# Borders of the feed forward and the embedding gate: memory homes, first banks and queue order of the next stage's preparations

## The chip, the cores and the metric

The kernel runs on one core of a Trainium2 chip. The metric is the device time of one execution in microseconds (us). A core has five engines with a queue each: TensorE (PE), VectorE (DVE), ScalarE (ACT), GpSimd (POOL) and SyncE (SP), which here issues all transfers. Each works through its queue in order; instructions of different queues wait for one another by semaphores. Products land in PSUM, eight banks of 128 x 512 float32; all else is in SBUF, 224 KB per partition.

## The reference

A block of two layers on 1024 tokens of width 1024, in float32. Layer 0 mixes tokens with a gated convolution beside attention over the 256 best keys of each query, layer 1 with a gated delta rule. After its mixer each layer has a feed forward and an embedding gate:

```python
for i in range(DEPTH):
    hn = rmsnorm(h, norm_mix_g[i])
    h = h + mixer(hn, ...)                      # layer 0: convolution and attention; layer 1: delta rule
    h = h + swiglu(rmsnorm(h, norm_ffn_g[i]), ffn_w_gate[i], ffn_w_up[i], ffn_w_down[i])
    e = rmsnorm(p[i] @ ple_w_proj[i], ple_post_norm_g[i])
    h = h + e * jax.nn.sigmoid(rmsnorm(h, ple_norm_g[i]) @ ple_w_gate[i])
```

`swiglu(h, g, u, d)` is `(silu(h @ g) * (h @ u)) @ d`, with an inner width of 2816.

## The kernel before

**Precision.** Every large product is made of three products of halves: `split` (lines 107 to 109) has ACT round a tile to a high half and DVE subtract it from the source for the low half.

**Feed forward, gate and up (`ffn`, `ffn_gu`).** The products of 2 x 2 blocks are made with seven block products instead of eight. The normalized rows, transposed and split, give eight operands: B11, B21, B22 and the sums T1 to T4 (T1 = B12 - B11 and so on), each a pair of 8 KB tiles. `right` lays each pair out in a pool of its own. Weights come by `weights(n)` for the blocks n = 0 to 21: a load into one of two buffers `wr`, four POOL sums (`wino`, lines 779 to 781), then splits by ACT and DVE. `group(n, x)` runs the seven products on the bank tiles a, b and c and sums them on ACT and DVE; line 867 is the sum that must have read bank a before the product with T4 may add to it. `first_group` does the same for n = 0 while it still transposes the operands (line 882). For each pair of blocks j = 0 to 10, lines 931 to 933 multiply the gate by the up part; line 933 reads the last bank a. The result goes to DRAM (gfD) with four POOL sums Sg.

**Feed forward, down (`ffn_down`).** Four units of 2, 3, 3 and 3 inner pairs, each of seven steps. A step loads its slot from gfD (line 997, SP), splits it (lines 1002 and 1003), adds the split weights (line 109), runs 6 or 9 products into each of four banks of chain a or b (line 1013), and moves the banks into h: the first time by an ACT copy (line 1018), later by a DVE addition (line 1016). The chains of the seven steps are a, b, b, a, b, a, a. The weights' sums T_dn are made on POOL. The slots s0, s1, s2 and a fourth are used in turn. Beside it, from the second unit on, one row tile per step of the residual is loaded from hB (line 1023) and added to h by POOL (line 1024).

**Embedding gate (`ple`).** `weights(u)` loads two buffers, has ACT round them (line 1111) and POOL subtract (line 1112), into w0 for u = 0 and w1a, w1b for u = 1. `norm(t)` scales a row tile by DVE (line 203), PE transposes it, and ACT and DVE split it into hh and hl. `gate(u, t, w)` runs 24 products per bank (line 1131), a sigmoid, a product with the loaded e and an addition into h. The norms of the even row tiles get the priority of the last step of down.

**What sets the order.** The builder walks the traced program by priority, which is the order of the source unless `high_priority` says otherwise, and puts each instruction into its engine's queue when, by its own model of the time, it is ready. So an instruction whose inputs are ready may stand ahead of older ones. `self.after([ins])` queues what its block traces on the engine of `ins` behind `ins`; it adds an order and no wait.

**Memory homes.** Pools are laid out one behind another on the left side of SBUF, others on the right. A new tile waits for the last users of the tiles that lay at its address. In layer 0, from address 19.9 KB on, the feed forward has (in KB, worked out by adding up the tile sizes): B11 19.9, T1 35.9, the split weights 51.9, T2 83.9, B21 99.9, the weights' sums 116.9, B22 132.9, the gate and up tiles 148.9, the tags Tb 166.9 and Ta 174.9. Attention had its output weights at 19.9 to 51.9 and kT at 68.4 to 100.4. Down then has, in layer 0: s0 19.9 to 43.9, raw weights 51.9 to 75.9, s1 83.9 to 107.9, s2 107.9 to 131.9, T_dn sums 132.9 to 148.9, the fourth slot 148.9 to 172.9. The embedding gate has w0 at 99.9 to 131.9 in both layers, on s1 and s2. PSUM: gate and up use two banks for a, two for b, four for transposes; down uses four for a and four for b, and the tag that a pool uses first gets the lower four.

## Time and profile before

| | |
|---|---|
| three executions | 2999.12, 3006.69 and 3008.4 us, median 3006.69 |
| profiled execution | 2999.78 us; its span from first to last instruction 2998.0 us |
| busy, share of the span | PE 96%, DVE 62%, ACT 42%, POOL 36% |
| mean granted clock of PE | 0.984 |
| chain that ended last | PE 76%, DVE 10%, POOL 4%, issue 3%, ACT 3%, DMA 3% |
| transfers | 340.80 MB, mean 114 GB/s |

The span is what the views of the trace cover; 1.8 us of the execution lie around it. A stretch of the trace is given in us from the start of the span. The stages in it: layer 0's mixer to about 690, gate and up to 1131, down to 1357, embedding gate to 1459, layer 1's mixer to 2220, gate and up to 2662, down to 2891, embedding gate to the end.

### The profile page before, as it was taken

The numbers are of one execution on the slowest core, as the hardware profiler recorded it, in microseconds if no ns is written. First come the engines' busy times: TensorE is split into PE (matmuls) and PEld (weight loads), VectorE is DVE, ScalarE is ACT, GpSimd is POOL, SyncE is SP. The second block draws the span as 40 slices with busy tenths as digits, with TensorE's granted clock in tenths as the row PEclk, the third lists the DMA queues.
The fourth block names the chain that finished last, engine by engine and source line by source line (L and its number), as shares of the span: only waits on it lengthen the run. The fifth ranks groups of instructions, "written<-read, shape, count | busy, mean of one in ns | idle before, by whom it ended". The sixth has DMA issues, their size and how long they took to land.

```text
span 2998.0 us, 47759 instructions
## 1 busy us (share of the span) xinstructions
PE 2873.8 (96%) x19211; PEld 2391.8 (80%) x19211; DVE 1870.4 (62%) x3274; ACT 1255.2 (42%) x2225; POOL 1072.6 (36%) x931
## 2 busy tenths in 40 slices
PE   7999998999999998999999999999999999999999
PEld 6989876787888886787887777788678888877877
DVE  5799995565444448974466767664455444469861
ACT  4467725454333334333444455443233333344341
POOL 1341000123444437525212443342144444466342
PEclk9999999999999999999999999999999999999999
DMA  4122165201322236523332232223612322255422
GB/s 145 50 50 92 57 197 203 86 22 39 113 105 102 106 119 217 188 95 121 103 124 101 93 110 97 90 92 119 253 63 78 107 104 106 105 194 192 144 72 95
DMA packets 119822, 340.80 MB, mean 114 GB/s; under 512 B 11696, under 2 KB 34608, under 8 KB 101936
## 3 DMA queue, kind: packets, MB, share of 16 engines
q1 hardware_dynamic: 119600, 337.74, 32.8%
q8 instruction: 151, 2.47, 0.3%
q14 instruction: 71, 0.58, 0.1%
HBM read 240.64 MB, written 97.06 MB: 113 GB/s over the span
## 4 chain that ended last, share of the span: by engine, by line
PE 76%; DVE 10%; POOL 4%; issue 3%; ACT 3%; DMA 3%; SPq 0%; DVEq 0%; ACTq 0%; POOLq 0%
PE pga L850 16%; PE pgb L850 8%; PE pso L1362 7%; PE pda L1013 6%; PE pdb L1013 5%; PE psp L1131 5%; PE psz L216 4%; PE pgc L850 4%; PE psow L237 3%; PE psz L1622 2%; PE pskqv L227 2%; PE y L742 2%; PE pswob L237 2%; DVE sc L467 1%; PE pse L1043 1%
## 5 line engine op out<-in xcount | busy, mean ns | idle before, releaser
L1013 PE MATMUL pda<-sl 128*128 128x512 f32 x1008 | 237.9, 394 | 19.1 <-DVE g L933 7.4
L1013 PEld LDWEIGHTS pda<-sl 128*128 128x128 f32 x1008 | 190.3, 190 | 63.1 <-DVE g L933 8.3
L781 POOL TENSOR_TENSOR S<-wr_gu 128x512 f32<-128x512 f32 x44 | 68.4, 1555 | 398.1 <-DMA wr_gu<-in_w_gu_dram 380.5
L1013 PE MATMUL pdb<-sl 128*128 128x512 f32 x792 | 185.4, 392 | 1.3 <-DVE h L1016 1.3
L1013 PEld LDWEIGHTS pdb<-sl 128*128 128x128 f32 x792 | 149.8, 189 | 33.9 <-DVE h L1016 1.3
L109 DVE TENSOR_TENSOR w2l_gu<-S,w2h_gu 128x1024 fp32r<-128x1024 f32 x44 | 66.7, 1517 | 165.0 <-ACT w2h_gu L108 164.8
L1362 PE MATMUL pso<-hh,wl_od 128*128 128x512 f32 x384 | 157.6, 410 | 0.0
L1362 PE MATMUL pso<-hh,wh_od 128*128 128x512 f32 x384 | 156.8, 408 | 0.0
L1362 PE MATMUL pso<-hl,wh_od 128*128 128x512 f32 x384 | 156.6, 408 | 0.0
L1002 ACT CAST sl<-sl 128x1536 fp32r<-128x1536 f32 (+1 forms) x54 | 74.7, 1386 | 134.4 <-DMA sl<-gfD 134.3
L108 ACT CAST w2h_gu<-S 128x1024 fp32r<-128x1024 f32 x44 | 46.2, 1051 | 188.6 <-PE pga L850 94.0
L1003 DVE TENSOR_TENSOR sl<-sl 128x1536 fp32r<-128x1536 f32 (+1 forms) x54 | 107.7, 1999 | 27.9 <-ACT sl L1002 27.6
L1380 DVE SCALAR_TENSOR_TENSOR c<-pso,odcw,c 128x509 f32<-128x509 f32 (+1 forms) x144 | 107.0, 743 | 26.1 <-ACT c L1377 24.3
L779 POOL TENSOR_TENSOR T_dn<-wr_dn 128x512 f32<-128x512 f32 x44 | 78.7, 1817 | 97.5 <-PE pgb L850 52.3
L227 PE MATMUL pskqv<-wh_kqv,hh 128*128 128x256 f32 x384 | 109.5, 285 | 0.3 <-ACT wh_kqv L108 0.3
L227 PE MATMUL pskqv<-wh_kqv,hl 128*128 128x256 f32 x384 | 108.7, 283 | 0.0
L227 PE MATMUL pskqv<-wl_kqv,hh 128*128 128x256 f32 x384 | 108.3, 283 | 0.0
L603 DVE TENSOR_SCALAR_CACHE_REDUCE tk_junk<-sc,tk_f 128x1024 int8<-128x1024 f32 (+5 forms) x111 | 102.5, 924 | 1.8
L153 POOL TENSOR_SCALAR nss_f<-nss_f 128x1 f32<-128x1 f32 x16 | 3.1, 192 | 276.0 <-ACT junk_f L152 276.0
L1131 PE MATMUL psp<-wh_pg,hh_p 128*128 128x512 f32 x256 | 101.6, 397 | 0.0
L1131 PE MATMUL psp<-wl_pg,hh_p 128*128 128x512 f32 x256 | 100.5, 392 | 0.0
L1131 PE MATMUL psp<-wh_pg,hl_p 128*128 128x512 f32 x256 | 100.3, 392 | 0.0
(543 smaller groups left out, 9027.3 us busy)
## 6 DMA issues: line engine op xcount, KB each, us to landing
wr_gu<-in_w_gu_dram SPq DMA_DIRECT2D x44, 1024.0 KB
sl<-gfD SPq DMA_DIRECT2D x42, 768.0 KB
gfD<-Sg SPq DMA_DIRECT2D x22, 1024.0 KB
wr_dn<-in_w_dn_dram SPq DMA_DIRECT2D x22, 1024.0 KB
wr_od<-in_w_qkv_dram SPq DMA_DIRECT2D x12, 1024.0 KB
cD<-c SPq DMA_DIRECT2D x24, 512.0 KB
gfD<-g SPq DMA_DIRECT2D x22, 512.0 KB
wr_z<-in_w_z_dram SPq DMA_DIRECT2D x10, 1024.0 KB
```

What stands on the lines that cost most here:

```text
L216: nc.tensor.matmul(ps[:M, f * 512:(f + 1) * 512], a[:, kc, c], b[f][:, kc, :], start=(kc == 0 and i == 0), stop=(kc == KC - 1 and i == 2))
L227: nc.tensor.matmul(out, a[:, kc, c], b[:, kc, :], start=(kc == 0 and i == 0), stop=(kc == KC - 1 and i == 2))
L237: nc.tensor.matmul(ps[:, f * 512:(f + 1) * 512], a[:, kc, tsl], b[:, f * 512:(f + 1) * 512], start=(kc == 0 and i == 0), stop=(kc == nk - ...
L603: v.tensor_scalar(jk[:, :n], sc[b], fb, 0.0, op0=op, op1=ALU.add, accum_out=c)
L779: sub = lambda o, x, y: eng.tensor_tensor(o, x, y, op=ALU.subtract)
L850: nc.tensor.matmul(bank, a[:, kc, :], b[:, kc, :], start=first and kc == 0 and m == 0, stop=kc == 3 and m == 2, skip_group_check=True)
L1002: nc.scalar.copy(y, x.bitcast(F32))
L1003: v.tensor_tensor(x, x.bitcast(F32), y.bitcast(F32), op=ALU.subtract)
L1013: nc.tensor.matmul(ps, a[:, i, c], b[:, i, :], start=first and i == 0 and k == 0, stop=i == m - 1 and k == 2, skip_group_check=True)
L1131: nc.tensor.matmul(ps, a[:, kc, c], b, start=kc == 0 and i == 0, stop=kc == KC - 1 and i == 2)
L1362: nc.tensor.matmul(ps[:, f * 512:(f + 1) * 512], a[:, kc, :], b[f][:, kc, :], start=(kc == 0 and i == 0), stop=(kc == KC - 1 and i == 2))
L1380: nc.vector.scalar_tensor_tensor(c[:, e:(f + 1) * 512], ps[:, e - d:(f + 1) * 512 - d], cw[:, k:k + 1], c[:, e:(f + 1) * 512], op0=ALU.mul ...
```

## The change

1. Layer 0's attention remembers its last copy of transposed probabilities (`last_pT`, on DVE), and `first_group` of layer 0 traces `weights(0)` behind it.
2. In layer 0 the operand pairs change places: T1 and T2 at 19.9 to 51.9, B11 and B21 at 83.9 to 115.9. Layer 1 keeps its order.
3. The tags Ta and Tb of gate and up get a pool each, in the same order.
4. In the last pair of blocks, lines 931 and 932 are queued behind the last group's line 867 (`last_sum`).
5. In down, the four banks of chain b of the first unit are taken before those of chain a.
6. The residual rows are loaded and added at the overall steps 9, 11, ... 23 instead of 7 to 14.
7. The embedding gate lays its pools out in the order hh0, hl0, hh1, hl1, w1a, w1b, e, a pad, w0, in both layers. In layer 0 that puts w1a at 83.9, w1b at 99.9, e at 115.9 and w0 at 132.9 to 164.9 KB; layer 1 has the same addresses, since both start at 19.9.

```diff
-                        eng(pT[:, q4:q4 + m, :].rearrange("p a b -> p (a b)"), p[:, :m * P])
+                        mark = eng(pT[:, q4:q4 + m, :].rearrange("p a b -> p (a b)"), p[:, :m * P])
+                    self.last_pT = mark.ins
...
-            right(("B11", "T1"), "h1")
+            right(("B11", "T1") if l else ("T1", "T2"), "h1")
             if not l:
                 self.W2 = self.pool(es, f"ffn{l}w")
-            right(("T2", "B21"), "h2")
+            right(("T2", "B21") if l else ("B11", "B21"), "h2")
...
-            tp_ = self.pool(es, f"ffn{l}t")
-            self.ffn_gu(sp, fp, tp_, l, H, gD, right)
+            tb_ = self.pool(es, f"ffn{l}t")
+            ta_ = self.pool(es, f"ffn{l}u")
+            self.ffn_gu(sp, fp, {"Ta": ta_, "Tb": tb_}, l, H, gD, right)
...
-            w1, w2 = weights(0)
+            with self.after(None if l else [self.last_pT]):
+                w1, w2 = weights(0)
...
-            v.tensor_tensor(g[:, 0], u[:, 0], g[:, 0], op=ALU.mult)
-            v.tensor_tensor(g[:, 1, 1], u[:, 1, 1], g[:, 1, 1], op=ALU.mult)
+            with self.after([self.last_sum] if j == NFF // 2 - 1 else None):
+                v.tensor_tensor(g[:, 0], u[:, 0], g[:, 0], op=ALU.mult)
+                v.tensor_tensor(g[:, 1, 1], u[:, 1, 1], g[:, 1, 1], op=ALU.mult)
             v.tensor_tensor(g[:, 1, 0], last, g[:, 1, 0], op=ALU.mult)
...
             banks = {}
+            if not ui:
+                for tp in range(4):
+                    banks["b", tp] = self.tp(f"pdb{l}_0_1_{tp}", "b")
...
-                    if first:
+                    if first and (ui or chain == "a"):
                         banks[chain, tp] = self.tp(f"pd{chain}{nm}_{tp}", chain)
...
-                t = next(rest, None) if ui else None
+                t = next(rest, None) if 7 * ui + si in range(9, 25, 2) else None
...
-            hh = [x("hh0")]
-            fp = mk("e")
-            if l:
-                w1 = [mk("w1a")]
-                hl = [x("hl0")]
-                self.pad(es, 8, f"plp0{l}")
-            else:
-                self.pad(es, 8, f"plp0{l}")
-                hl = [x("hl0")]
-                w1 = [mk("w1a")]
+            hh, hl = [x("hh0")], [x("hl0")]
             hh.append(x("hh1"))
-            w0 = mk("w0")
-            self.pad(es, 1, f"plp1{l}")
             hl.append(x("hl1"))
             hT = [hh, hl]
-            w1.append(mk("w1b"))
+            w1 = [mk("w1a"), mk("w1b")]
+            fp = mk("e")
+            self.pad(es, 9, f"plp0{l}")
+            w0 = mk("w0")
```

## Rows read from the trace of the kernel before

**Rows 1.** Busy time of each engine over the span, from the page.

```profile
PE 2873.8 (96%) x19211; PEld 2391.8 (80%) x19211; DVE 1870.4 (62%) x3274; ACT 1255.2 (42%) x2225; POOL 1072.6 (36%) x931
```

**Rows 2.** Waits of PE over the span: engine line, waited for, us in total, times, longest us.

```profile
PE tp_p L193 <- DVE hn_p L203: 9.5, 6, 2.2
...
PE pda L1013 <- DVE g L933: 7.4, 2, 6.9
...
PE pda L1013 <- DVE h L1016: 7.4, 7, 2.7
...
PE tp_f_B L882 <- DVE HB11l L109: 5.4, 3, 2.0
...
PE pda L1013 <- ACT h L1018: 3.3, 1, 3.3
```

**Rows 3.** Stretches: us, length, busy by engine (rows 1's order), PEclk, DMA share, GB/s.

```profile
670.95:684.60 13.65, 11.22 (x41) 9.80 (x42) 4.33 (x7) 2.48 (x3) 5.13 (x4) 0.50 0.23 78
...
1138.58:1148.82 10.24, 6.20 (x15) 4.90 (x16) 5.35 (x7) 1.62 (x3) 9.62 (x8) 0.50 0.40 132
...
1363.86:1367.27 3.41, 2.89 (x11) 2.70 (x12) 3.41 (x7) 1.47 (x3) 3.41 (x2) 0.50 0.87 308
...
2691.64:2698.47 6.83, 5.06 (x12) 4.00 (x13) 5.62 (x6) 2.88 (x6) 5.99 (x4) 0.50 0.98 312
...
2896.44:2903.27 6.83, 4.94 (x16) 4.26 (x17) 6.62 (x9) 4.39 (x8) 6.67 (x5) 0.50 0.47 155
```

**Rows 4.** Timeline, attention to feed forward, layer 0: start, us, instruction, count, idle before.

```profile
667.37 2.23 DVE L109 TENSOR_TENSOR w1l_gu<-wr_gu,w1h_gu 128x1024 fp32r<-128x1024 f32 x1
...
671.92 1.12 PE L734 MATMUL tpp<-cf,L 128*128 128x128 f32 x4 [2.49 <-DVE pT L736]
...
672.83 5.22 PE L742 MATMUL y<-vv,pT 128*128 128x64 f32 x24
...
678.09 0.69 DVE L675 TENSOR_TENSOR yR<-y,ri 128x512 f32<-128x512 f32 x1 [4.32 <-PE y L742]
```

**Rows 5.** Timeline, gate and up to down, layer 0, DVE and PE.

```profile
1126.36 1.59 DVE L931 TENSOR_TENSOR g<-u,g 128x1024 f32<-128x1024 f32 x1
...
1127.88 0.68 DVE L867 TENSOR_TENSOR u<-pga,u 128x512 f32<-128x512 f32 x1
...
1128.61 0.50 PE L850 MATMUL pga<-HT4h,w2h_gu 128*128 128x512 f32 x1 [2.05 <-DVE u L867]
...
1131.48 4.27 PE L1013 MATMUL pda<-sl 128*128 128x512 f32 x18
...
1141.89 0.68 DVE L933 TENSOR_TENSOR g<-pga,g 128x512 f32<-128x512 f32 x1
...
1142.62 2.93 PE L1013 MATMUL pda<-sl 128*128 128x512 f32 x6 [6.88 <-DVE g L933]
...
1146.72 0.69 DVE L109 TENSOR_TENSOR sl<-wr_dn,sl 128x512 fp32r<-128x512 f32 x1 [4.16 <-ACT sl L108]
```

**Rows 6.** Stretches as in 3, over both down borders and the later units.

```profile
1124.87:1193.40 68.53, 56.88 (x235) 45.69 (x234) 61.32 (x55) 31.88 (x48) 57.09 (x30) 0.93 0.59 209
...
2657.61:2717.20 59.59, 49.94 (x193) 38.23 (x192) 57.17 (x47) 26.95 (x42) 51.94 (x28) 0.91 0.67 237
...
1264.00:1345.00 81.00, 81.00 (x359) 67.11 (x358) 62.08 (x75) 33.16 (x43) 19.06 (x16) 1.00 0.32 101
```

**Rows 7.** By line: count, duration ns min/median/max, first and last start us.

```profile
L1024 POOL TENSOR_TENSOR h<-h,hres x16: 2389/2748/3917, 1179.6 to 2781.3; 128x1024 f32<-128x1024 f32 x16
...
L1016 DVE TENSOR_TENSOR h<-pdb,h x88: 673/679/693, 1148.1 to 2875.1; 128x512 f32<-128x512 f32 x88
```

**Rows 8.** Timeline, down to the embedding gate, layer 0, DVE and POOL.

```profile
1337.86 1.28 DVE L203 SCALAR_TENSOR_TENSOR hn_p<-h,ss_p,gB_pn 128x1024 f32<-128x1024 f32 x1
...
1357.58 11.36 POOL L1112 TENSOR_TENSOR wl_pg<-wr_pg,wh_pg 128x1024 fp32r<-128x1024 f32 x4 [13.55 <-issue]
...
1358.41 5.92 DVE L203 SCALAR_TENSOR_TENSOR hn_p<-h,ss_p,gB_pn 128x1024 f32<-128x1024 f32 x2 [0.24 <-PE tp_p L193]
```

More of the change, by code (lines that the diff above doesn't have):

```diff
@@ L885, in sums @@
             def sums(n, tag, f):
-                T = tmp(tp_, f"T_f{l}_{n}", tag)
+                T = tmp(tp_[tag], f"T_f{l}_{n}", tag)
                 for p in range(NT // 2):
@@ L923, in ffn_gu @@
         for j in range(NFF // 2):
-            g = (tmp(tp_, f"g{l}_{j}", "Ta") if j % 2 else tmp(fp, f"g{l}_{j}", "g")).rearrange("p (a b) n -> p a b n", a=2)
+            g = (tmp(tp_["Ta"], f"g{l}_{j}", "Ta") if j % 2 else tmp(fp, f"g{l}_{j}", "g")).rearrange("p (a b) n -> p a b n", a=2)
             last = group(2 * j, g) if j else first_group(g)
@@ L930, in ffn_gu @@
             last = group(2 * j + 1, u)
-            v.tensor_tensor(g[:, 0], u[:, 0], g[:, 0], op=ALU.mult)
-            v.tensor_tensor(g[:, 1, 1], u[:, 1, 1], g[:, 1, 1], op=ALU.mult)
+            with self.after([self.last_sum] if j == NFF // 2 - 1 else None):
+                v.tensor_tensor(g[:, 0], u[:, 0], g[:, 0], op=ALU.mult)
+                v.tensor_tensor(g[:, 1, 1], u[:, 1, 1], g[:, 1, 1], op=ALU.mult)
             v.tensor_tensor(g[:, 1, 0], last, g[:, 1, 0], op=ALU.mult)
-            S = tmp(tp_, f"Sg{l}_{j}", "Tb")
+            S = tmp(tp_["Tb"], f"Sg{l}_{j}", "Tb")
             self.wino(gp, [S[:, i] for i in range(4)], [g[:, 0, 0], g[:, 1, 0], g[:, 0, 1], g[:, 1, 1]], "left")
```

## Prediction

> **What bounds the kernel now.** I read the page's busy times first: TensorE (PE) is busy for 2873.8 of 2998.0 us [rows 1], so all that a change of order and memory can win is the 124 us in which PE does nothing, and what its low clock costs. Next the list of who waited for whom, PE alone [rows 2]: the reader is to see that its entries name the borders. Products of the down projection (line 1013) wait for the last product of the gate (line 933), and for additions into h (line 1016); transposes of the embedding gate wait for its normalized rows (line 203); transposes of the feed forward wait for the low half of B11. Third the granted clock by stretches [rows 3]: after each of these borders it is 0.50, that is 1.2 GHz instead of 2.4, for 3.4 to 13.65 us. PE at the low level does half the work, so a stretch costs at most half of PE's busy time in it. Last the timelines at each border, engine by engine [rows 4, 5, 8], with VectorE's busy share over the borders [rows 6], since VectorE (DVE) is what most of these waits name.
>
> **Attention to feed forward, layer 0.** Before, two splits of the first weights (the first is shown, 2.23 us at 667.37) run on DVE ahead of a copy of transposed probabilities that PE waits for: 2.49 us idle [rows 4]. The change queues all DVE work of weights(0) behind the last such copy. That gap goes whole, as DVE has nothing else ahead of the copy: -2.5. The two splits (2.23, the second at the same rate for its half, 1.7 estimated) now stand after the last copy and perhaps before yR. The 24 products into y took 5.22 at the low level, so about 2.6 at the high one; 3.9 of splits less the part that runs beside them, 2.3, may hold yR by 0 to 1.6: I take +1.6, since the splits are ready first. Behind yR on DVE nothing else is urgent; who waits for it is PE's transposes tpy. The clock was low from 670.95 for 13.65 us with 11.22 us of PE work [rows 3]: 0 to 5.6 us to be had. The idle before it goes, a shorter one at yR stays, so I take half, -2.8. B11 gets the memory of attention's kT, whose last reader is the last logits product, in place of the output weights, whose last reader is attention's last product: its split can follow its transposes at once. In question is the wait for HB11l, 5.4 us in three waits, one of them in layer 1 [rows 2], so 0 to some 3.4: I take -1.5, since ScalarE also has the last row's square to do there. T1 and T2 go where B11 and T1 were; their splits come later than the last attention product anyway: 0. Sum -5.2, between -0.9 (the gap less the splits) and -11.5 (2.5, 5.6 and 3.4).
>
> **Gate and up to down, layer 0.** Three edits meet. (1) Line 931 (1.59 us) ran ahead of line 867, for which PE's last four-term product waited 2.05 us [rows 5]; queued behind it, the wait is line 867 itself, 0.69: -1.4. Behind the held multiplication are only the output's own sums, needed much later. (2) Chain b is given its banks first, so chain a of the down projection falls on the four banks that held transposes and have long been free. The trace shows what this is worth: chain a ran 18 products, three banks of six, and then waited 6.88 us for line 933 to read the fourth, low clock after it [rows 5]. Now step 0's 24 products and 18 of step 1 can run before that bank is asked for; 24 more at 4.27/18 = 0.237 are 5.7 us, so 1.2 of 6.88 remains, moved to chain b. (3) The low clock after it, 10.24 us with 6.20 of PE work, costs up to 3.1 [rows 3]. PE could so win 1.4 + 5.7 + 3.1 = 10.2, and the next wait for line 1016 besides. But DVE decides: over 1124.87 to 1193.40 it is busy 61.32 of 68.53 us [rows 6], and what PE needs next comes from it. Its largest idle, 4.16 us at 1146.72 [rows 5], waits for a slot that step 0 frees, and step 0 now ends earlier. If all its idle closes, DVE and so PE arrive 68.53 - 61.32 = 7.2 us earlier, less about 1.2 of that at the stretch's end where DVE waited for PE's pace: -6.0, between 0 and -10.2. The new homes put T2 under the first slot, so its load is issued up to 12 products (2.8 us) later; the slot is completed only by the second pair's weights, whose buffer the last weights of the gate free, so I cost it at nothing, and at 2.8 if that cover is gone. Splitting the pool of Ta and Tb keeps both addresses (8 KB each, in the same order): 0.
>
> **The same border, layer 1.** Here line 933 cost PE only the 0.5 left of 7.4 [rows 2] and DVE is busy 57.17 of 59.59 [rows 6]: -2.4, between 0 and -8.2 (the 2.4, the 3.3 that PE waited for a ScalarE copy of h [rows 2], and half of 5.06 at the low clock [rows 3]).
>
> **Residual rows.** Eight loads of hB and eight POOL additions per layer (16 in all, 2.39 to 3.92 us, median 2.75 [rows 7]) ran on steps 7 to 14 and now run on every second step from 9 to 23. Each load is an instruction in SyncE's queue that also holds the slot loads; moved past them it can hold that queue only when its buffer of two is not free, and two steps between adds make that rarer. A DVE operation with both inputs in SBUF slows beside POOL: line 203 from 1.28 to 2.96 us each [rows 8]. So an addition costs DVE about 2.75 x (1 - 1.28/2.96) = 1.6 us. Line 1016, with one input in PSUM, stays at 0.67 to 0.69 whatever POOL does [rows 7]. In question are the waits for line 1016, 7.4 us, of which 2.7 is the one in layer 0's first unit counted above [rows 2]; of the other 4.7 I take half, -2.3 over both layers, between -4.7 and 0. The four additions that move to the later units cost DVE 6.4 us per layer there, where it is idle for 81.0 - 62.1 = 18.9 us [rows 6]; without that cover they would be PE's. The Trainium skill, SBUF — State Buffer, section "Who interferes with whom", says that GpSimd and a DVE instruction with two SBUF inputs exclude each other for a whole instruction, and that one with one SBUF input is not touched. The trace agrees with the second half (line 1016 stays at 0.69); by the first the price of an addition would be its whole 2.75, and the four would take 11 us of that idle instead of 6.4.
>
> **Down to the embedding gate, both layers.** Before, w0's low halves lie on the slot of the very last step; POOL's four subtractions (11.36 us) start only at 1357.58, when the last product is done, and the two row scalings that PE's transposes need take 5.92 beside them instead of 2 x 1.28 [rows 8]. After, w0 lies on the T buffers of down and on the slot of the step before the last, 36 products (8.1 us, 81.0/359 each [rows 6]) earlier. Two of four conversions can run before the last two steps, two during the last. So DVE is alone at the border: 5.92 - 2.57 = -3.4 per layer, -6.8 in both, of the 9.5 us that PE waits there [rows 2]. The low clock after it covers 2.89 and 4.94 us of PE work [rows 3]: up to -3.9, I take half, -2.0. The e tiles lie on the last slot now and load later; only POOL's product after the first gate needs them: 0, and the time of one load if it is late, on a chain that PE does not wait for. Swapped chains also mean that the first transposes meet other banks of chain a: 0 to 0.7 (one line 1016 [rows 7]) per layer. Sum -8.8, between 0 and -13.4 (9.5 and 3.9).
>
> **Sum.** 5.2 + 6.0 + 2.4 + 2.3 + 8.8 = 24.7 us. The profiled execution took 2999.78 and would take 2975.1; it lies 6.9 under the median of the three runs shown, 3006.69, from which the same sum gives 2982.0. I forecast 2982.
>
> **Rivals.** (a) The clock falls at these borders all the same, for they still consist of transposes and short waits. Then the halves that I took go, 2.8 + 2.0: 2986.8. For it: in rows 3 the low stretches lie where transposes and gaps alternate; against: gaps shrink from 2.49 and 2.2 to under 1. The Trainium skill, TensorE: Matmul & The Clock Gate, section "Part 4: PE-mode transpose", says that transposes do not count as busy for the clock as products do, which would make this rival the case. (b) DVE holds the down projection: its order keeps line 933 behind the same preparations, and chain b waits where chain a did. The border terms of down and the residual rows fall away (10.7): 2992.7. For it: 57.17 of 59.59 [rows 6]. (c) With that, the conversions of w1, whose buffers w0 now frees earlier, move onto the border and slow line 203 as w0 did; the gate's 8.8 go too and 5.2 is left: 3001.5, no change. Against: w1's second half lies on the last slot. (d) Slower: the later residual additions meet POOL's T sums for the last unit, on steps where DVE has no idle; SyncE's queue stands at the next hres load. It decides from the point where DVE needs over 8.1 us per step. Eight moved additions (four per layer) at the longest, 3.92, cost 31.4, and with only the 5.2 and 8.8 gained the time is 3006.7 + 31.4 - 14.0 = 3024. (e) More than the sum: all low stretches of rows 3 go and the terms come at their better bounds for attention and the gate (11.5 + 13.4 + 10.7): 2971. That the edges do not bind (the builder would have ordered so anyway) is part of (b).
>
> **How the numbers follow.** Forecast 0.33, (a) 0.12, (b) 0.17, (c) 0.19, (d) 0.08, (e) 0.11. A measurement of this kernel tells a change of about 0.3%, 9 us, from none. Faster by more: forecast, (a), (b), (e) = 0.73; within: (c) = 0.19; slower: (d) = 0.08. The range goes from 2966, a little under (e) as DVE's better bound in layer 0 is not in it, to 3003, just over (c); (d) lies outside.
>
> **What would show it.** Right: no PE wait for line 736 before the last y products; the four-term product waiting under 1 us; no wait of chain a for line 933; POOL's line 1112 done before the last product of down, line 203 at 1.28 there; fewer low stretches. Wrong: a new PE wait of over 3 us in the units of down that names line 1016 or 1003, line 203 still near 3 us, or chain b waiting for line 933 as long as chain a did.

## The result and the profile after

| | before | changed |
|---|---|---|
| median of the executions | 3007.27 us | 2990.58 us |
| ratio, 95% interval | | 0.995 (0.9934 to 0.9965) |
| profiled execution; span | 2999.78; 2998.0 us | 2983.25; 2981.5 us |
| mean granted clock of PE | 0.984 | 0.987 |

The change makes the kernel 16.7 us faster by the medians, and the two profiled spans differ by 16.5; both profiled executions lie some 7 us under their medians. The forecast was 24.7 less, so the direction and the range (2966 to 3003) held and the size came out at two thirds. The page of the changed kernel, in the columns of [rows 1]:

```profile
PE 2868.9 (96%) x19211; PEld 2387.9 (80%) x19211; DVE 1871.5 (63%) x3274; ACT 1256.5 (42%) x2226; POOL 1062.8 (36%) x931
```

PE's busy time fell by 4.9 us only, for the same 19211 products, so nearly 12 of the 16.5 are PE waits and the rest is low clock. The reader is to see in the next view, waits of PE (us in total, times, longest), what became of the entries of [rows 2]:

```profile
PE pda L1020 <- DVE h L1023: 14.2, 5, 6.4
...
PE tp_p L193 <- DVE hn_p L203: 6.5, 4, 2.7
...
PE tp_f_B L885 <- DVE HB11l L109: 5.4, 3, 2.0
...
PE pda L1020 <- DVE slw L109: 4.6, 3, 3.1
...
PE tpy L681 <- DVE yR L675: 2.7, 1, 2.7
```

The wait of chain a for the last product of the gate (7.4 us, line 933 before, 937 after) is gone from the list, and chain a's waits for additions into h (line 1016 before, 1023 after) nearly doubled from 7.4 to 14.2. The waits for normalized rows fell from 9.5 to 6.5. The waits for HB11l are what they were. One grew: 2.7 for yR, 0.8 before.

Where the time went is read best by stages. The rows u2 to u7 undo one part of the change each, by its number; b7 is the kernel before with part 7 alone; n4, n12, n124, x and v12 alter the changed kernel further. Part 1 was not undone by itself. The table is worked out from the timelines: the start of the first instruction of a stage (transposes of the feed forward, products of down, transposes of the gate, products of layer 1's mixer) taken from the start of the next. "Gate 0" runs to the products pso of layer 1's mixer, some 30 us after the gate's end. "Tail" is from attention's last logits product.

| us | tail | gate/up 0 | down 0 | gate 0 | mixer 1 | gate/up 1 | down 1 | gate 1 |
|---|---|---|---|---|---|---|---|---|
| before | 24.4 | 443.4 | 225.8 | 137.2 | 723.8 | 444.2 | 228.8 | 106.8 |
| changed | 20.8 | 441.6 | 229.1 | 128.6 | 724.1 | 444.2 | 225.9 | 103.2 |
| u2 operand homes undone | 21.1 | 442.1 | 232.3 | 130.1 | 725.2 | 444.2 | 225.7 | 105.9 |
| u3 pools of Ta, Tb undone | 21.2 | 441.7 | 234.8 | 131.7 | 722.9 | 444.2 | 227.1 | 104.7 |
| u4 edge on 931, 932 undone | 21.1 | 441.7 | 229.1 | 131.2 | 722.2 | 444.2 | 227.4 | 104.6 |
| u5 banks undone | 20.9 | 441.6 | 229.7 | 130.1 | 722.1 | 444.2 | 225.8 | 103.2 |
| u6 residual steps undone | 21.1 | 441.7 | 231.2 | 130.2 | 723.2 | 444.2 | 228.6 | 104.7 |
| u7 gate homes undone | 21.0 | 441.7 | 229.8 | 137.6 | 727.3 | 444.2 | 226.4 | 106.7 |
| b7 before, gate homes alone | 23.3 | 445.1 | 227.3 | 130.1 | 725.2 | 444.2 | 228.7 | 103.2 |
| n4 additions first | 20.9 | 441.6 | 227.8 | 131.6 | 722.1 | 444.1 | 224.6 | 104.7 |
| n12 splits and halves held | 16.9 | 441.6 | 228.9 | 130.4 | 722.8 | 444.2 | 227.9 | 103.6 |
| n124 all three orders | 18.4 | 441.6 | 226.4 | 130.5 | 725.4 | 445.7 | 223.7 | 103.6 |
| x sums on ScalarE | 21.1 | 441.7 | 214.5 | 131.5 | 725.5 | 444.1 | 212.0 | 105.8 |
| v12 sums on VectorE | 16.9 | 442.1 | 229.9 | 130.5 | 721.7 | 444.2 | 228.7 | 103.6 |

Changed less before: -3.6 in the tail, -1.8 in gate and up, **+3.3 in down of layer 0**, **-8.7 in gate 0**, -2.9 in down of layer 1, -3.6 in gate 1. A profile is one execution: what lies ahead of the tail took 663.7 to 670.6 us in these kernels though no edit touches it, mixer 1 spreads by 5.6, and gate 0 of the kernels with new homes by 3.1, with the low clock in it or not. The changed kernel, u4, u5, u7 and n12 have nearly the same queue in down; they agree within 0.9 us in down 0 and 2.2 in down 1, and the tail of an unaltered order within 0.4. The kernel before moves more: b7, whose queues are the same as before's up to the end of layer 0's down, took 23.3 in the tail, 445.1 in gate and up and 227.3 in down. Against b7 the -3.6, -1.8 and +3.3 are -2.5, -3.5 and +1.8. Differences of stages are read against that, and whole kernels by their ratios.

Down can be cut further by counting its products: its first unit has 168, its second 252. In layer 0 the first unit takes 51.4 us before (52.9 in b7) and 56.3 after; the second takes 60.1 and 58.3; the last two together 114.4 both times. So the +3.3 are 4.9 lost in the first unit and 1.7 won in the second.

**The tail.** Timeline of DVE and PE:

```profile
671.71 2.02 DVE L109 TENSOR_TENSOR w1l_gu<-wr_gu,w1h_gu 128x1024 fp32r<-128x1024 f32 x1
...
673.65 1.74 DVE L109 TENSOR_TENSOR w2l_gu<-wr_gu,w2h_gu 128x512 fp32r<-128x512 f32 x1
...
675.32 0.68 DVE L675 TENSOR_TENSOR yR<-y,ri 128x512 f32<-128x512 f32 x1
...
676.05 1.12 PE L681 MATMUL tpy<-cf,yR 128*128 128x128 f32 x4 [2.70 <-DVE yR L675]
```

The copies of probabilities have DVE to themselves now and the 2.49 us of [rows 4] are gone. The two splits stand ahead of yR, and PE waits 2.70 for it where it waited 0.78. The low clock covers 6.83 us instead of 13.65:

```profile
674.20:681.02 6.82, 4.30 (x12) 3.22 (x13) 3.71 (x4) 2.48 (x3) 2.32 (x2) 0.50 0.46 154
...
1141.82:1152.06 10.24, 8.71 (x19) 5.92 (x20) 10.24 (x10) 3.15 (x5) 10.24 (x7) 0.50 0.62 222
...
1172.54:1179.37 6.83, 3.89 (x9) 3.13 (x10) 6.83 (x8) 3.36 (x6) 5.01 (x3) 0.50 0.23 85
...
1355.58:1363.00 7.42, 4.19 (x35) 3.68 (x34) 6.98 (x8) 6.45 (x12) 4.69 (x2) 1.00 0.64 202
...
2694.89:2701.71 6.82, 3.78 (x9) 3.07 (x10) 6.82 (x7) 3.87 (x6) 6.35 (x5) 0.50 0.21 79
```

These are stretches as in [rows 3]. At the border to the gate in layer 0 (fourth line) the clock is 1.00 throughout; in down of layer 0 it is 0.50 twice.

**Gate and up to down, layer 0.** Timeline, PE and DVE:

```profile
1123.66 0.50 PE L852 MATMUL pga<-HT4h,w2h_gu 128*128 128x512 f32 x1 [0.32 <-DVE u L869]
...
1137.71 1.66 PE L1020 MATMUL pdb<-sl 128*128 128x512 f32 x6 [1.46 <-DVE g L937]
...
1142.67 0.79 PE L1020 MATMUL pda<-slw,sly 128*128 128x512 f32 x1 [3.06 <-DVE slw L109]
...
1165.55 4.61 DVE L1010 TENSOR_TENSOR sl<-sl 128x1536 fp32r<-128x1536 f32 x2 [0.46 <-ACT sl L1009]
...
1171.28 3.45 DVE L109 TENSOR_TENSOR sl<-wr_dn,sl 128x512 fp32r<-128x512 f32 x2
...
1174.66 0.68 DVE L1023 TENSOR_TENSOR h<-pda,h 128x512 f32<-128x512 f32 x1
...
1175.48 2.90 PE L1020 MATMUL pda<-sl 128*128 128x512 f32 x6 [5.73 <-DVE h L1023]
```

Two waits of [rows 5] are smaller: 2.05 became 0.32, and the 6.88 for the last product of the gate became 1.46, now on chain b. Then PE waits 3.06 for the splits slw and 5.73 for the addition of step 5's first bank (2.72 at the same place before, in the view below). And 1175.48, where that wait ends, is just 1.8 us ahead of the place it ended before, though down began 5.0 us ahead; the low clock from 1172.54 takes those 1.8 back by the second unit's first product. The addition's six products were done by about 1165.6 (24 take 5.6 us from 1164.2 on); DVE did 4.61 and 3.45 us of preparations first.

```profile
1177.27 5.76 PE L1013 MATMUL pda<-sl 128*128 128x512 f32 x24 [2.72 <-DVE h L1016]
```

**Down to the gate.** Timeline, layer 0, POOL, DVE, PE:

```profile
1348.75 4.75 POOL L1111 TENSOR_TENSOR wl_pg<-wr_pg,wh_pg 128x1024 fp32r<-128x1024 f32 x2 [1.56 <-ACT wh_pg L1110]
...
1358.31 5.70 POOL L1111 TENSOR_TENSOR wl_pg<-wr_pg,wh_pg 128x1024 fp32r<-128x1024 f32 x2 [4.81 <-ACT wh_pg L1110]
...
1356.71 1.28 DVE L203 SCALAR_TENSOR_TENSOR hn_p<-h,ss_p,gB_pn 128x1024 f32<-128x1024 f32 x1 [0.24 <-PE tp_p L193]
...
1359.11 2.65 DVE L203 SCALAR_TENSOR_TENSOR hn_p<-h,ss_p,gB_pn 128x1024 f32<-128x1024 f32 x1
...
1358.05 1.09 PE L193 MATMUL tp_p<-cf,hn_p 128*128 128x128 f32 x8 [0.56 <-DVE hn_p L203]
...
1361.81 1.09 PE L193 MATMUL tp_p<-cf,hn_p 128*128 128x128 f32 x8 [2.67 <-DVE hn_p L203]
```

w0's subtractions are over before the last product, and the third row's scaling takes 1.28. But 5.70 us of POOL for w1 start at 1358.31 and the fourth scaling takes 2.65 beside them. PE waits 0.56 and 2.67 instead of 1.90 and 2.20. From the first transposes to the first gate product it is 7.07 us, before 8.72: 1.65 less, in both layers. To the last gate product another 1.9 is won in each layer: in layer 0 a wait of 1.14 at 1386.14, and in both the low clock of [rows 3]'s third and fifth stretch. The other 5.1 of gate 0's 8.7 us lie at the start of layer 1's mixer, and u7 and b7 show why.

### The profile page after: what moved, and what is told of

The parts are those of the page before. It is cut to its first block, busy times and chain, and to the rows that moved or that the text cites. A ratio compares the mean times of both kernels' runs of the same rounds, so it can differ in the third digit from the quotient of the medians.

```text
span 2981.5 us, 47762 instructions
## 1 busy us (share of the span) xinstructions
PE 2868.9 (96%) x19211; PEld 2387.9 (80%) x19211; DVE 1871.5 (63%) x3274; ACT 1256.5 (42%) x2226; POOL 1062.8 (36%) x931
## 4 chain that ended last, share of the span: by engine, by line
PE 78%; DVE 10%; POOL 3%; DMA 3%; ACT 3%; issue 2%; SPq 0%; DVEq 0%; ACTq 0%; POOLq 0%
PE pga L852 16%; PE pgb L852 8%; PE pso L1361 7%; PE psp L1130 6%; PE pda L1020 6%; PE pdb L1020 4%; PE psz L216 4%; PE pgc L852 4%; PE psow L237 3%; PE psz L1621 2%; PE pskqv L227 2%; POOL T_dn L780 2%; PE y L743 2%; DVE sc L467 1%; PE pswob L237 1%
## 5 line engine op out<-in xcount | busy, mean ns | idle before, releaser
L1020 PE MATMUL pda<-sl 128*128 128x512 f32 x1008 | 236.5, 393 | 15.2 <-DVE h L1023 14.2
L780 POOL TENSOR_TENSOR T_dn<-wr_dn 128x512 f32<-128x512 f32 x44 | 82.8, 1908 | 115.9 <-DVE sl L109 61.1
```

Source lines behind the costliest of these rows:

```text
L780: sub = lambda o, x, y: eng.tensor_tensor(o, x, y, op=ALU.subtract)
L1020: nc.tensor.matmul(ps, a[:, i, c], b[:, i, :], start=first and i == 0 and k == 0, stop=i == m - 1 and k == 2, skip_group_check=True)
```

## The experiments

Each kernel but b7 is the changed kernel with one more edit, so line numbers shift by a few between them. Ratios are to the kernel before; the changed kernel's is 0.995.

**u7: the gate's homes undone.** The pools of the embedding gate go back to their old order.

```diff
-            hh, hl = [x("hh0")], [x("hl0")]
-            hh.append(x("hh1"))
-            hl.append(x("hl1"))
+            hh = [x("hh0")]
+            fp = mk("e")
...
+            hh.append(x("hh1"))
+            w0 = mk("w0")
+            self.pad(es, 1, f"plp1{l}")
+            hl.append(x("hl1"))
             hT = [hh, hl]
-            w1 = [mk("w1a"), mk("w1b")]
-            fp = mk("e")
-            self.pad(es, 9, f"plp0{l}")
-            w0 = mk("w0")
+            w1.append(mk("w1b"))
```

> The changed kernel with part 7 undone (the embedding gate's pools in their old order, both layers). Theory N (homes of the stage after): the order moved hl1 and the second half of the gate's weights off the place where layer 1's mixer lays its split z and ab weights; with the old order these splits wait for the last gate product again. 10 to 11 us slower than the changed kernel: about 1.6 at each border from down to the gate, 5 to 7 at the border from the gate to layer 1's mixer (ScalarE's rounding of zabh at the end of the gate instead of some 45 us earlier, PE waits of about 2 and 3 us there), about 2 in layer 1's gate. Rival P (the prediction's term, the border from down to the gate alone): 3.3 slower if the border is worth what the trace of after shows there, 8.8 if it is worth what was forecast, and no difference in the first 20 us of layer 1's mixer.

Measured: 0.998 (0.997 to 0.9989). In the table gate 0 goes back to 137.6 and gate 1 to 106.7, before's values. Timeline of u7 at the end of gate 0, ScalarE and PE, and the same rounding in the changed kernel:

```profile
1464.20 1.98 ACT L108 CAST zabh<-wr_z 128x1024 fp32r<-128x1024 f32 x2
...
1467.41 0.39 PE L227 MATMUL pszab<-zabh,hh 128*128 128x272 f32 x1 [2.05 <-ACT zabh L108]
...
1471.16 1.94 PE L193 MATMUL tp_n<-cf,hn_n 128*128 128x128 f32 x8 [3.37 <-DVE hl L109]
```

```profile
1410.62 1.99 ACT L108 CAST zabh<-wr_z 128x1024 fp32r<-128x1024 f32 x2
```

zabh and zabl, the split weights of layer 1's mixer, lie at 138.5 to 155.5 KB in all these kernels (from adding up the tiles). In the old order hl1 and the second half of w1 lie there, which PE reads to the end of the gate; in the new order it is w0, which is done when half of the gate is. So the rounding runs some 50 us earlier, beside the gate, and two waits at the start of the mixer (2.05 and 3.37) become one of 2.00. Low clock of 6.83 us followed the two waits (at 1462.85 before); behind the one it is 3.41 us or none in all kernels with the new homes. Theory N is borne out.

**b7: the gate's homes alone**, the same edit made in the kernel before.

> The kernel before with part 7 alone (the embedding gate's pools in the new order). Theory N (homes of the stage after): this part carries most of the change: 11 to 13 us faster than before, of which 3.3 at the two borders from down to the gate, 3.8 inside the gates, 5 to 6 at the start of layer 1's mixer. Rival P (the borders alone): 3.3 to 8.8.

Measured: 0.9968 (0.9956 to 0.998), some 10 us of the change's 15. Gate 0 takes 130.1 (7.1 less than before) and gate 1 103.2 (3.6 less). The rounding of zabh starts at 1416.88. N again; the borders from down to the gate, with waits of 0.56 and 2.67, give 1.65 each as in the changed kernel.

**u5: the banks undone.**

```diff
-            if not ui:
-                for tp in range(4):
-                    banks["b", tp] = self.tp(f"pdb{l}_0_1_{tp}", "b")
...
-                    if first and (ui or chain == "a"):
+                    if first:
```

> The changed kernel with part 5 undone (chain a takes its four banks before chain b). Theory D (VectorE's order decides the first unit of down): PE waits some 5 to 6 us for line 937 in chain a again, but the last products of the first unit, which wait for the additions into h, start within 1 us of where they start in the changed kernel; the whole time is within 2.5 us of it. Rival P (the banks are worth what was forecast): 5.7 us slower in layer 0, kept to the end.

Measured: 0.9946 (0.9933 to 0.9959). Timeline of PE (the addition into h is line 1020 here):

```profile
1134.50 2.93 PE L1017 MATMUL pda<-sl 128*128 128x512 f32 x6 [2.64 <-DVE u L871]
...
1140.07 2.25 PE L1017 MATMUL pda<-sl 128*128 128x512 f32 x6 [2.64 <-DVE g L937]
...
1178.06 1.19 PE L1017 MATMUL pda<-sl 128*128 128x512 f32 x2 [7.30 <-DVE h L1020]
```

Chain a waits for gate and up again, 2.64 twice, then the wait for the addition is 7.30 instead of 5.73 and without the one for slw. The first unit takes 56.4 us in layer 0, against 56.3, and down 229.7 and 225.8, against 229.1 and 225.9. So the 5.7 us forecast for the banks are worth under 1: theory D.

**u4: the edge on lines 931 and 932 undone.**

```diff
-            with self.after([self.last_sum] if j == NFF // 2 - 1 else None):
+            with self.after(None):
```

> The changed kernel with part 4 undone (the gate's two multiplications of the last pair are not queued behind the last group's sum). Theory D (VectorE decides the first units of down): the edge moved 2.3 us of VectorE's work, lines 931 and 932 of before and the sum of bank b, from the time of PE's last gate products into the stretch where VectorE is the bound. Undone, the four-term product waits 2.05 us again and down starts 1.7 later, but the first product of the second unit starts 1 to 4 us earlier than in the changed kernel in layer 0. Rival P (as forecast): down starts 1.7 us later and all of it stays, 1.4 to 1.8 slower at the second unit.

Measured: 0.9949 (0.9935 to 0.9964), and neither theory: PE still waits 0.32 us there, gate and up takes 441.7 as in the changed kernel. The queue of VectorE is the same in both kernels, instruction for instruction: with the other parts in place the builder orders it so without the edge. The 1.8 us gained there belong to some combination of the others (PE waits 0.78 in u2, 0.38 in u3); which, stays open. The queues of the other engines are the same too, so this profile is in effect a second execution of the changed kernel. It differs by 2.7 us in gate 0, 1.9 in mixer 1, 1.5 in down 1 and 1.4 in gate 1.

**u2: the operand homes of layer 0 undone.**

```diff
-            right(("B11", "T1") if l else ("T1", "T2"), "h1")
+            right(("B11", "T1"), "h1")
...
-            right(("T2", "B21") if l else ("B11", "B21"), "h2")
+            right(("T2", "B21"), "h2")
```

> The changed kernel with part 2 undone (B11 and T1 at 19.9 to 51.9, T2 and B21 at 83.9 to 115.9 in layer 0). Rival P (as forecast): the two waits for HB11l (1.95 and 1.40 us) would be longer by 1.5 in all. Theory Q (these waits are ScalarE's and VectorE's own order: the last row's square and scale stand between the splits): they stay at 1.95 and 1.40, and feed forward starts within 0.3 us of where it does. At the border from gate and up to down the first slot's load may come up to 2.8 us earlier or not; the second unit starts within 3 us of the changed kernel's, earlier if the homes of T2 hold the slots back.

Measured: 0.9962 (0.995 to 0.9974). The waits for HB11l stay at 1.95 and 1.40 and the tail at 21.1: theory Q, no memory was in question there. But down of layer 0 is 3.3 us longer. Timeline of PE in down, then of DVE:

```profile
1144.60 1.83 PE L1020 MATMUL pdb<-sl 128*128 128x512 f32 x6 [3.99 <-DVE g L937]
...
1173.01 6.20 PE L1020 MATMUL pda<-sl 128*128 128x512 f32 x19 [3.19 <-DVE sl L1010]
...
1182.73 2.31 PE L1020 MATMUL pda<-sl 128*128 128x512 f32 x6 [3.53 <-DVE h L1023]
...
1164.38 1.29 DVE L109 TENSOR_TENSOR sl<-T_dn,sl 128x512 fp32r<-128x512 f32 x2 [6.81 <-ACT sl L108]
```

Chain b waits 3.99 for the gate's last product instead of 1.46, and step 6 waits 3.19 for its slot (line 1010). DVE stands 6.81 us at a split into the fourth slot, where the changed kernel has 1.54. The fourth slot lies on the last pair's sums Sg, and ScalarE waits 7.85 us there until their write to DRAM has landed (1.34 in the changed kernel). So the homes act on the order of down's queues, where the forecast had them at nothing, or at 2.8 lost.

**u3: one pool for Ta and Tb.**

```diff
-            tb_ = self.pool(es, f"ffn{l}t")
-            ta_ = self.pool(es, f"ffn{l}u")
-            self.ffn_gu(sp, fp, {"Ta": ta_, "Tb": tb_}, l, H, gD, right)
+            tp_ = self.pool(es, f"ffn{l}t")
+            self.ffn_gu(sp, fp, {"Ta": tp_, "Tb": tp_}, l, H, gD, right)
```

> The changed kernel with part 3 undone (the tags Ta and Tb share one pool, addresses as in the changed kernel). Rival P (as forecast): nothing, since both addresses stay; within 1 us at every stage. Theory R (a shared pool changes what the tiles behind it wait for, and so the order of VectorE's queue): the splits into slw, which lie on Ta, stand 15 instructions later in VectorE's queue and preparations of the second unit stand ahead of the first unit's last; the second unit of down starts at another time than in the changed kernel by more than 2 us in at least one layer. From the two waits for slw (3.06 us in layer 0) the direction is open: between 5 us earlier and 5 us later.

Measured: 0.9962 (0.9949 to 0.9974). Down 0 takes 234.8 (5.7 more); down 1 with 227.1 is within what executions differ. No address differs, but the queue of VectorE does: the splits into slw stand 13 places later, behind other preparations. Timeline of PE in down 0:

```profile
1148.16 13.81 PE L1019 MATMUL pdb<-sl 128*128 128x512 f32 x48 [3.98 <-DVE h L1022]
...
1165.16 0.50 PE L1019 MATMUL pda<-slw,sly 128*128 128x512 f32 x1 [2.26 <-DVE slw L109]
...
1175.13 8.57 PE L1019 MATMUL pda<-sl 128*128 128x512 f32 x24 [5.05 <-ACT h L1024]
...
1242.02 3.27 PE L1019 MATMUL pda<-sl 128*128 128x512 f32 x8 [3.41 <-DVE h L1022]
```

Four waits, 14.7 us; all waits in these two units are 16.4, and 11.8 in the changed kernel. Theory R: the pool is what the tiles behind it wait for, and the builder's order follows.

**u6: the residual rows at their old steps.**

```diff
-                t = next(rest, None) if 7 * ui + si in range(9, 25, 2) else None
+                t = next(rest, None) if ui else None
```

> The changed kernel with part 6 undone (residual rows loaded and added at steps 7 to 14). If the residual rows are what shortened the waits for the additions into h in the second unit, three waits of 0.6 to 0.9 us come back in each layer where the changed kernel has one, 1.3 to 1.9 us per layer, 2.6 to 3.8 in all. If those waits shortened because the chains swapped banks, nothing changes (within 1 us).

Measured: 0.9962 (0.9948 to 0.9975). Timeline of PE, end of the second unit of down 0, then three splits of DVE there, and the same three in the changed kernel:

```profile
1233.86 4.36 PE L1020 MATMUL pda<-sl 128*128 128x512 f32 x18 [0.90 <-DVE h L1023]
...
1238.88 4.40 PE L1020 MATMUL pda<-sl 128*128 128x512 f32 x18 [0.66 <-DVE h L1023]
...
1244.18 6.14 PE L1020 MATMUL pda<-sl 128*128 128x512 f32 x26 [0.90 <-ACT sl L108]
...
1239.35 4.09 DVE L109 TENSOR_TENSOR sl<-T_dn,sl 128x512 fp32r<-128x512 f32 x3
```

```profile
1237.12 1.88 DVE L109 TENSOR_TENSOR sl<-T_dn,sl 128x512 fp32r<-128x512 f32 x3
```

The three short waits of before are back where the changed kernel has one of 0.91. The queue of VectorE is the same in both kernels; the splits take 4.09 beside two of POOL's additions and 1.88 without them. Down is 2.1 longer in layer 0 and 2.7 in layer 1, of which the second unit makes 2.0 in each (60.3 us against 58.3); so the later steps are worth 4.1 in both.

**n4: additions first.**

```diff
-                with self.after([self.last_sum] if ui == 0 and si else None):
+                with self.after([self.last_sum] if ui == 0 and si else [self.step5] if ui == 1 and si < 2 else None):
...
-                        v.tensor_tensor(hv, ps, hv, op=ALU.add)
+                        add = v.tensor_tensor(hv, ps, hv, op=ALU.add)
+                        if (ui, si) == (0, 5):
+                            self.step5 = add.ins
```

> The changed kernel, and in down the VectorE preparations of the first two steps of the second unit are queued behind the additions into h of the first unit's step 5 (counted from 0). Theory D (order on VectorE): the waits of 5.73 us (layer 0) and 6.42 us (layer 1) for line 1023 fall under 3 us each, and the low clock after them goes: 3 to 7 us per layer, 6 to 12 faster than the changed kernel. Rival W (VectorE's whole work decides, whatever its order): the wait moves to the first products of the second unit, which start within 1 us of where they did; the time changes by less than 2 us.

Measured: 0.9935 (0.9922 to 0.9948). Timeline of PE:

```profile
1176.58 4.36 PE L1020 MATMUL pda<-sl 128*128 128x512 f32 x18 [0.87 <-DVE h L1023]
...
1235.36 5.04 PE L1020 MATMUL pda<-sl 128*128 128x512 f32 x14 [4.10 <-DVE h L1023]
```

The 5.73 fell to 0.87, but 58 us later a wait of 0.91 grew to 4.10. In layer 0 the first unit is 6.6 us shorter and the second 4.8 longer; down is shorter by 1.3 and 1.2 us. Mostly rival W: within the first two units the work of VectorE decides, and its order moves the wait about.

**x: the weights' sums taken off GpSimd** (copies on ScalarE in their place, so this kernel leaves the sums out of its result).

```diff
-                self.wino(gp, [T[:, i] for i in range(4)], [q[:, i] for i in range(4)], "right")
+                if ui < 2:
+                    for i in range(4):
+                        nc.scalar.copy(T[:, i], q[:, i])
+                else:
+                    self.wino(gp, [T[:, i] for i in range(4)], [q[:, i] for i in range(4)], "right")
```

> The changed kernel, but the five weights' sums of the first two units of down (twenty GpSimd operations per layer) are replaced by twenty ScalarE copies of the raw blocks, so these sums are left out of what is computed. Theory G (VectorE is the bound of the first units because GpSimd works beside it): VectorE's preparations there fall from 1.7 and 2.3 us to 0.7 and 1.2, the waits of 5.73 and 6.42 us for line 1023 fall under 2 us each, and the third unit starts 5 to 9 us earlier in layer 0 and 4 to 8 in layer 1. Rival (VectorE's own count of instructions is the bound): the waits move by less than 2 us.

Measured: 0.9856 (0.9842 to 0.987). Stretches as in [rows 3], from the last group's sum to the second unit's first product, in x and in the changed kernel:

```profile
1129.80:1174.92 45.12, 42.20 (x183) 33.67 (x181) 36.18 (x47) 35.77 (x61) 13.80 (x8) 1.00 0.74 277
```

```profile
1122.91:1182.84 59.93, 48.68 (x182) 37.38 (x181) 54.84 (x48) 26.15 (x41) 48.94 (x28) 0.86 0.57 209
```

For the same work but one split (1.24 us, at the end of the second stretch) DVE is busy 36.18 us instead of 54.84 once POOL is busy 13.80 instead of 48.94. PE's waits there fall to 0.83 and 1.77, no low clock is left, and down takes 214.5 and 212.0: 14.6 and 13.9 us less. Theory G: the first units of down are held by VectorE, and VectorE by GpSimd's sums beside it. One thing else changed with it and was not tried apart: with POOL free the last pair's sums are done 12.1 us after down's first product instead of 30.4, and the copies are ready sooner than the sums were.

**n12: two orders more.** VectorE's first splits behind the last yl, and GpSimd's subtractions for w1 behind the first odd row's norm.

```diff
-            with self.after(None if l else [self.last_pT]):
+            with self.after(None if l else [self.last_yl]):
...
+                        with self.after([self.odd] if u else None):
+                            gp.tensor_tensor(wt[1][:, i:i + 2], r, wt[0][:, i:i + 2].bitcast(F32), op=ALU.subtract)
```

> The changed kernel with two orders more. (i) VectorE's splits of layer 0's first feed forward weights are queued behind the last yl instead of the last copy of probabilities. If they are what holds yR, its wait falls from 2.70 to about 0.8 us and the low clock there gets shorter: 1.9 to 4 us. (ii) GpSimd's four subtractions of the gate's second weights are queued behind the first odd row's norm. If they are what slows the last even row's scaling (2.65 us), it takes 1.28 and PE waits 1.2 to 1.5 us less at both borders from down to the gate. Sum 4 to 7 us faster than the changed kernel. Rival: the waits stay, the scaling is held by something else; no change.

Measured: 0.9939 (0.9926 to 0.9951). Timeline, the wait for yR, then the fourth scaling, the subtractions and PE's wait at the gate:

```profile
677.29 0.66 PE L681 MATMUL tpy<-cf,yR 128*128 128x128 f32 x4 [0.78 <-DVE yR L675]
...
1358.20 1.27 DVE L203 SCALAR_TENSOR_TENSOR hn_p<-h,ss_p,gB_pn 128x1024 f32<-128x1024 f32 x1
...
1361.17 5.75 POOL L1112 TENSOR_TENSOR wl_pg<-wr_pg,wh_pg 128x1024 fp32r<-128x1024 f32 x2
...
1359.53 1.95 PE L193 MATMUL tp_p<-cf,hn_p 128*128 128x128 f32 x8 [1.30 <-DVE hn_p L203]
```

yR's wait is 0.78, no low clock is left at it, and the tail takes 16.9, 4 us less. The scaling takes 1.27 and the wait for it 1.30 instead of 2.67. Both mechanisms are as named. By the ratio the gain over the changed kernel lies within the intervals of both.

**n124: these two and n4's.**

> The changed kernel with the three orders together: layer 0's first feed forward splits behind the last yl, the gate's second low halves behind the first odd row's norm, and the second unit's first two preparations behind the additions of step 5. From the runs that had them apart: 4.0 in attention's tail, 1.3 at each border from down to the gate, 1.2 to 1.8 in each down: 8 to 10 us faster than the changed kernel if they add up. Rival: they share their gains, since VectorE and GpSimd have the same work in all; 4 to 6.

Measured: 0.9935 (0.9923 to 0.9947). Tail 18.4, down 226.4 and 223.7. The intervals of n4, n12, n124 and the changed kernel overlap: faster than before all, better than the changed kernel not shown.

**v12: n12 with the sums on VectorE.** In the first two units of both layers wino is given VectorE instead of GpSimd, in the first unit queued behind the last group's sum.

> The changed kernel with the first two orders (first feed forward splits behind the last yl, the gate's second low halves behind the first odd row's norm), and in both layers the five weights' sums of the first two units of down (twenty operations) made on VectorE instead of GpSimd, those of the first unit behind the last group's sum. Theory G (GpSimd beside it slows VectorE by more than the sums cost VectorE itself): twenty sums at 0.6 to 0.7 us cost VectorE 12 to 14 us, and leaving them off GpSimd gave PE 14.7 and 13.2 us with 9 us of VectorE idle left in the first unit of layer 0; so the third unit starts 4 to 10 us earlier than in the changed kernel in each layer, and with 4.0 and twice 1.3 for the two orders the whole is 14 to 26 us faster than the changed kernel. Rival: the exclusion is symmetric, what GpSimd no longer holds VectorE now does itself; within 3 us in down, 6 faster in all.

Measured: 0.9936 (0.9923 to 0.995); down takes 229.9 and 228.7, no better than the changed kernel. Timeline, DVE, PE and ScalarE:

```profile
1156.09 0.69 DVE L109 TENSOR_TENSOR sl<-T_dn,sl 128x512 fp32r<-128x512 f32 x1 [6.22 <-ACT sl L108]
...
1157.44 4.70 PE L1021 MATMUL pdb<-sl 128*128 128x512 f32 x12 [5.33 <-DVE h L1024]
...
1155.44 1.14 ACT L108 CAST sl<-T_dn 128x512 fp32r<-128x512 f32 x2 [15.29 <-DMA gfD<-Sg]
```

DVE stands 6.22 us at a split whose source ScalarE had not rounded yet, with two finished products' additions queued behind it, and PE waits 5.33 for the second of them; in layer 1 it is 6.76 and 9.02. ScalarE had stood 15.29 us (15.26 in layer 1) for the write of the last pair's sums, on whose place that slot lies. So it isn't settled what the sums would cost on VectorE in another order. The rival's time came out, but the view shows queues held at their heads by that write.

## Why the prediction was right, and where not

**What bounds it** was right: the time is in the borders, PE's busy time changed by 4.9 us, and nearly every term that moved names DVE; the exception is ScalarE's rounding of zabh. Of the signs named beforehand, one of being wrong came: a new PE wait of over 3 us in down that names the additions into h, 5.73 us in layer 0 and 6.42 in layer 1.

**Attention's tail:** forecast -5.2, measured -3.6 (-2.5 against b7). The 2.49 went whole, and the two splits held yR by 1.9 more (forecast 1.6): right. Of the low clock 6.83 us stayed, as assumed. The term that failed is B11's new home, forecast -1.5: the waits for HB11l are 1.95 and 1.40, old home or new (before, changed, u2). The doubt that stood beside it, the last row's square and scale, is the cause that fits; that part wasn't tried.

**Gate and up to down, layer 0:** forecast -6.0, with a part of the residual rows' -2.3. Measured -1.8 ahead of down and +3.3 in it (-3.5 and +1.8 against b7). The step that failed is "If all its idle closes, DVE and so PE arrive 68.53 - 61.32 = 7.2 us earlier". PE's first wait fell as forecast (6.88 to 1.46), but in the first unit of down DVE is busy 51.2 of 56.3 us now, where it was busy 45.4 of 51.4. Its busy time isn't a fixed sum that PE can ask for earlier: which split stands ahead of which addition, and whether GpSimd runs beside it, decides when an addition is done. Undoing the banks moves nothing (u5); removing GpSimd's sums moves 14.6 (x). Rival (b) had the mechanism, "DVE holds the down projection", and put the wait at chain b and line 933; it came at line 1023. The edge, forecast at -1.4, does nothing by itself (u4). What stands behind it, "only the output's own sums, needed much later", left out that the fourth slot lies on these sums: they are written 30.4 us after down's first product instead of 22.3, and a split into the slot waits for that write. It costs ScalarE 1.34 us in the changed kernel, but 7.85 in u2 and 15.29 in v12. Splitting the pool, forecast at 0, is worth 5.7 us in layer 0 (u3), and the operand homes, costed here at nothing, are worth 3.3 (u2): same addresses or far places, but another order in VectorE's queue. These parts don't add up: undone alone, parts 2, 3 and 6 cost 11.1 us in down 0, yet down 0 of the kernel before, without any of them, is 3.3 shorter than with all (1.8 in b7).

**Layer 1's border and the residual rows:** forecast -2.4 and a share of -2.3; measured -2.9 in down 1, with 2.2 between executions. The second unit makes 1.95 of it. The first unit fell from 54.1 to 52.8 us, but kernels with the same queue take 52.8 to 54.9 there, so a gain at this border is not shown. The residual rows by themselves are worth 2.0 in each layer (u6), 4.1 where 2.3 was forecast: right in mechanism, as DVE's splits in u6 show, and inside its bounds of 0 and 4.7. The four additions that moved to later units cost nothing there, as said: in layer 0 the last two units take 114.4 us as before.

**Down to the gate:** forecast -8.8 in both layers, measured -7.2 (twice 1.65 and 1.9), but in other proportions. The waits named in [rows 2], 9.5 us, fell by 3.0 where 6.8 was taken: the conversions of w1 took w0's place, as rival (c) had it. Its contrary reason, that w1's second half lies on the last slot, left out that the first half does not, and two of its subtractions (5.70 us) are enough to slow one scaling to 2.65. The rest, 4.2 where 2.0 was taken, is nearly all low clock: half of the 2.89 and 4.94 us that PE worked in it is 3.9. The Trainium skill, SBUF — State Buffer, section "Who interferes with whom", has a VectorE instruction with two SBUF inputs contend with a GpSimd instruction that reads SBUF, over shared ports that are an exclusive lock. The traces agree: a split of 512 columns takes 0.68 alone, a GpSimd sum of that size 1.30 alone (x), and each of them about 1.75, a little under the sum of both, where they alternate in the changed kernel.

**What no step had:** 5.1 us at the start of layer 1's mixer, whose weights took over the place that the gate freed (u7, b7). The prediction asked what a new home waits for, and never who waits for the old one. So the total was near partly for a poor reason: in layer 0's gate and up and down 7.15 were forecast (6.0, and half of the residual rows) and 1.5 were lost, 8.6 off (1.7 won and 5.5 off against b7), and 5.1 came in a stage that had no term.

**The clock:** rival (a) had it that the low stretches stay. At the borders to the gate the changed kernel's profile has none, but u5 and u4 have 3.4 and 6.8 us there at the same instructions, so the 4.2 is this execution's, and the half that was taken is not refuted. In the kernels with the new homes, leaving out those with n12's orders, the way to the first gate product is 7.1 us without low clock and 7.8 with it. The reason given against the rival, that the gaps shrink to under 1 us, did not hold: PE still waits 2.70 for yR and 2.67 at the gate.

## What to carry to other kernels

When a tile gets a new home, list both neighbours: whose end it now waits for, and what of the next stage waits for the place it left; here the second was worth 5.1 us beside the 7.2 of the first, a part of which was low clock. Where an in-order engine is busy 85 to 95% of a border, a shorter wait on PE is not a gain until the same engine's later waits have been followed for two more units, and an edit that changes no address can still change that engine's queue. Before moving work about on VectorE, look at what GpSimd does beside it.

## What the runs showed of the hardware

- How much GpSimd's work holds VectorE in the first units of down: 35.1 us of it less (48.94 to 13.80) took 18.7 us off VectorE's busy time (54.84 to 36.18), of which 1.24 are one split that only the longer stretch holds: 17.4 us for the same instructions, 0.50 us for each. The additions into h, with one input in PSUM, took 8.1 us in both. The price per us had been read rightly from line 203 (1.6 of 2.75), but set against the residual rows alone and not against the weights' sums.
- The clock's low stretches come and go between executions at the same instructions: behind the first transposes of gate 0 none in the changed kernel's profile, 3.41 us in u5, 6.83 in u4, whose queues are the same; a stage that holds one differs by up to 3 us from one that doesn't.
